# A two-layer hybrid backbone: S5 table arithmetic and its transfers put on other engines, modulation steps set after each weight chunk

## The chip, the cores and the metric

The kernel runs on one core of a Trainium2 chip. The metric is the device time of one execution in microseconds. A core has five engines that run side by side, each with a queue of its own: TensorE (PE, matmuls; PEld is its weight load), VectorE (DVE), ScalarE (ACT), GpSimd (POOL) and SyncE (SP), which here issues most transfers.

## What is computed

Two streams of 256 tokens (latents `x`, context `ctx`) of width 1024 pass through two layers. Each layer is a half-step SwiGLU feed-forward, a mixer of four branches (latent attention, Hyena convolution, S5 state space, neighbourhood attention) and a second half-step feed-forward. Every part is modulated by nine vectors that come from `c` (latents) and `c_ctx` (context):

```python
def ffn_sublayer(x, mods, base, g_pre, g_post, w_in, w_out):
    h = modulated_norm(x, g_pre, mods[base], mods[base + 1])
    return x + 0.5 * mods[base + 2] * rms_norm(swiglu(h, w_in, w_out), g_post)

mod_l = act_l @ w_mod[i] + b_mod[i]          # act_l = silu(c); 9 vectors of 1024
mod_c = act_c @ w_mod[i][:, :n_c] + b_mod[i][:n_c]   # 9 vectors in layer 0, 5 in layer 1
lam_bar = jnp.exp(lam_dt)                    # S5: powers of this make the tables
b_bar = ((lam_bar - 1.0) / lam)[..., None] * (b_re + 1j * b_im)
```

In layer 1 only the latents go through the mixer to the end, so its last four modulation vectors are needed for the latents alone.

## The kernel before

**Weight chunks.** Every weight chunk of 128 x 1024 is loaded by SP into one of four `raw` buffers and split into a high and a low part, `wh` on ScalarE (L220) and `wl` on VectorE (L221), each with three buffers. The product takes three matmuls per tile (L227 to L229). VectorE's, ScalarE's, GpSimd's and SP's instructions are put in order by a scheduler that simulates the program; only PE keeps the order of the code. `after(mark[...])` adds the rule that an instruction stands behind the marked one on its engine: `mark["wl"]` is the latest `wl`, `mark["wh"]` the latest `wh`.

**Feed-forward** (`ffn`, L533). 22 pairs of chunks, one pair a round `f`: `u[0]` and `u[1]` give the two halves, `gate` (L541 to L548) joins them on ScalarE (L543) and VectorE (L544, L545, split at L234). After each pair `step(2)` (L571) lets other work advance by two weights. The output projection calls `step(1)` after each of 16 chunks. There are four feed-forwards; three carry other work. A is layer 0's first, B layer 0's second, C layer 1's first.

**Modulation tiles** (`mod_flow`, L286). One 128 x 1024 tile of `w_mod` per step. The latents' sum is one VectorE operation (L328); the context's is a multiply on GpSimd (L332) and a sum on ScalarE (L306). In A (layer 0, vectors 2 to 8) the tiles come from SP through the same four `raw` buffers as the weights; from vector 5 on VectorE does both streams. In B and C (layer 1) they have a ring of two buffers of their own and GpSimd issues the loads (L298): vectors 0 to 4 in B, 5 to 8, latents alone, in C. In C even tiles go to VectorE, odd ones to GpSimd and ScalarE. `stepper` (L628) spreads the steps over the weights: 58 over 46 in A, 42 over 50 in B, 34 over 50 in C. In A each step also advances the Hyena filters (`hyg`, L798).

**Tables of layer 1's S5** (`s5_tables`, L1132), eight slices, 0 to 2 in B, 3 to 7 in C. `ahead` (L605) runs 4 steps a slice and 3 more over the first 15 rounds. A slice's steps:

1. On GpSimd the six small products `bb` (L1181) and the six products `wt` of 128 x 512 (L1183): the input weights.
2. On GpSimd six operations for the output vectors `vv` (L1187 to L1192); on VectorE the rotations (L1194); on ScalarE the decays (L1197). `toeplitz` of the slice before: eight small reads (L1159).
3. PE turns `wt` (L1206), ScalarE copies it to `rin`, which is stored (L1208). `keep` of the slice before (L1163).
4. PE multiplies `vv` and `bb` (L1217), which makes `strip`; `vv` is stored (L1231); the parameters of the next slice are loaded (`first`, L1146).

All transfers of this function are issued by GpSimd (`dma = G.dma_start`, L1137). Each table tile has one buffer. L205 to L210 are the six lines of the helper `cmul`, whatever engine calls it. Layer 0 makes the same tables in its own S5 part (`s5_lane`): there `wt` is made on VectorE (`prep2`) and the eight reads are issued by SP.

Of the kernel before, what the change touches and what calls it, by code (L numbers as in the profile page):

```python
# [9 lines left out]
F32 = mybir.dt.float32  # L10
# [6 lines left out]
P = 128  # L17
# [146 lines left out]
def build(tc, A):  # L164
# [20 lines left out]
    with st, tc.manual_schedule(engines={mybir.EngineType.PE}):  # L185
# [99 lines left out]
        def mod_flow(l, js, act, raw=None):  # L285

            if callable(act):
                act = act()  # L290
            tiles = [(j, k) for j in js for k in range(KT)]
            ws, back = {}, []

            def load(n):
                if n < len(tiles):
                    j, k = tiles[n]
                    ws[n] = raw() if raw else rp.tile([P, D], F32, tag="raw", name="raw")
                    (G.dma_start if raw else dma)(ws[n], A["wmod"][l, j, k])  # L298

            def finish():  # L300
                while back:
                    back.pop(0)()

            def sums(w, s, c):
                with after(mark["wh"]):
                    S.activation(w, w, AF.Copy, scale=0.5, accum_out=md[l][:, s, c : c + 1])  # L306

            def bias(j, ss):
                for s in ss:
                    m = md[l][:, s, j * KT : (j + 1) * KT]  # L310
                    V.tensor_tensor(m, m, bmt[l][:, j * KT : (j + 1) * KT], op=ALU.add)

            if raw:
                load(0)
                yield
            for n, (j, k) in enumerate(tiles):
                finish()
                load(n + 1 if raw else n)
                c = j * KT + k
                w = ws.pop(n)  # L320
                ss = [1] if l == 1 and j >= 5 else [0, 1]
                both = l == 0 and j >= JB
                fast = ss if both else [] if ss == [1] and k % 2 else [1]
                slow = [s for s in ss if s not in fast]
                for s in fast:
                    jk = sp.tile([P, D], BF16, tag="sq", name="jk", bufs=1)
                    with after(mark["wl"]):
                        V.scalar_tensor_tensor(  # L328
                            jk, w, 0.5, act[s], op0=ALU.mult, op1=ALU.mult, accum_out=md[l][:, s, c : c + 1]
                        )  # L330
                for s in slow:
                    G.tensor_tensor(w, w, act[s], op=ALU.mult)  # L332
                    back.append(lambda w=w, s=s, c=c: sums(w, s, c))
                if k == KT - 1:
                    back.append(lambda j=j, ss=ss: bias(j, ss))
                yield
            finish()

# [194 lines left out]
        def ffn(l, i, h, late, toks, nxt, gp, step, rows, fill, begun=(), xpool2=None):  # L533
# [16 lines left out]
            for f in range(NF):  # L550
                u = [new_unit(f, ab) for ab in range(2)]
                if late and f == 0:
# [11 lines left out]
                        return run  # L564

                    front([keep(u[0]), keep(u[1]), keep(u2[0])], late)
                elif late and f == 1:
                    gate(1, [pss[2], u2[1](None)])
                else:
                    gate(f, [v(None) for v in u])  # L570
                step(2)  # L571
                if f == NF - 3:
                    nxt["gr"] = rows()

# [30 lines left out]
        def ahead(stack, gp, name, slices):  # L605
# [14 lines left out]

            def go():
                f[0] += 1
                for _ in range(n * f[0] // 15 - n * (f[0] - 1) // 15):
                    next(gen, None)

            return go
# [35 lines left out]
        with ExitStack() as fs:  # L662
# [127 lines left out]
                        acts.extend(act_load())  # L790
                return acts

            st0 = stepper([(mod_flow(0, [2, 3, 4], acts0), 25), (mod_flow(0, [5, 6, 7, 8], acts0), 33)], 46, 6)

            def step0(w):
                st0(w)
                with after(mark["sp"], mark["dve"]):
                    next(hyg, None)  # L798

            late = ffn(0, 0, h, late, TALL, nxt, gp, step0, lambda: gate_rows(0, 0, 1, 0.5, [0, 1]), fill0, begun)  # L800
            h = nxt["h"]
# [2 lines left out]
        for l in range(L):  # L804
# [8 lines left out]
            with ExitStack() as fs:  # L813
# [4 lines left out]
                else:  # L818
# [6 lines left out]
                    st1 = stepper([(mod_flow(1, [0, 1, 2, 3, 4], act_load, raw1), 42)], 50, 2)  # L825
                    tg1 = ahead(fs, gp, "s5p", range(0, 3))

                    def step1(w):
# [5 lines left out]
            if not last:  # L834
                with ExitStack() as fs:
# [7 lines left out]
                    st2 = stepper([(mod_flow(1, [5, 6, 7, 8], act_load, raw2), 34)], 50, 2)  # L843
                    tg2 = ahead(fs, gp, "s5q", range(3, 8))

                    def step2(w):
# [285 lines left out]
def s5_tables(E, l, slices, tabd, sds, tp, py):  # L1132
# [10 lines left out]
    bh = lambda t, n: t.unsqueeze(2).to_broadcast([P, 4, n, 16])  # L1143
    b8 = lambda t: t.unsqueeze(3).to_broadcast([P, 4, 8, 8])
    b1 = lambda t: t.unsqueeze(2).to_broadcast([P, 4, 8, 8])
    def first(sl):  # L1146
        s5t = tp.tile([P, 4, S5_TAB], F32, tag="s5t", name="s5t")
        dma(s5t, E["s5d"][l][:, sl * 4 : sl * 4 + 4])
        prm = tp.tile([P, 5, 4, 16], F32, tag="prm", name="prm")
        dma(prm[:, 0:4], A["s5bc"][l, sl].rearrange("p a (x h) -> p a x h", h=16))  # L1150
        return s5_views(s5t), prm

    def strips(sl, strip):
# [2 lines left out]
    def toeplitz(sl):  # L1156
        tz = tp.tile([P, 4, P], F32, tag="tz", name="tz")
        for s in range(8):
            dma(tz[s * 16 : (s + 1) * 16], sds[sl][:, 0:16, (7 - s) * 16 : (7 - s) * 16 + 128].rearrange("q h d -> h q d"))  # L1159
        return tz  # L1160

    def keep(sl, tz):
# [1 line left out]

    slices = list(slices)
    s5, prm = first(slices[0])
    late = [lambda: None] * 3
    for i, sl in enumerate(slices):
        late[0]()
        rin = tp.tile([P, S5_IN], F32, tag="rin", name="rin")  # L1170
# [8 lines left out]
        h16 = lambda t: t.unsqueeze(2).to_broadcast([P, 4, 16])  # L1179
        G.tensor_scalar(prm[:, 4], prm[:, 3], -1.0, None, op0=ALU.mult)  # L1180
        cmul(G, bb[:, 0], bb[:, 1], prm[:, 0], prm[:, 1], h16(s5["kr"]), h16(s5["ki"]), tmp[:, :, 0])  # L1181
        wt = tp.tile([P, 2, 4, 8, 16], F32, tag="wt", name="wt")
        cmul(G, wt[:, 0], wt[:, 1], bk(s5["wr"], 8), bk(s5["wi"], 8), bh(bb[:, 0], 8), bh(bb[:, 1], 8), tmp[:, :, 0:8])  # L1183
        yield
        late[1]()
        vr, vi = bk(s5["vr"], 9), bk(s5["vi"], 9)
        G.tensor_tensor(vv[:, 0], vr, bh(prm[:, 2], 9), op=ALU.mult)  # L1187
        G.tensor_tensor(tmp, vi, bh(prm[:, 3], 9), op=ALU.mult)
        G.tensor_tensor(vv[:, 0], vv[:, 0], tmp, op=ALU.subtract)
        G.tensor_tensor(vv[:, 1], vr, bh(prm[:, 4], 9), op=ALU.mult)  # L1190
        G.tensor_tensor(tmp, vi, bh(prm[:, 2], 9), op=ALU.mult)
        G.tensor_tensor(vv[:, 1], vv[:, 1], tmp, op=ALU.subtract)  # L1192
        t4 = E["sp"].tile([P, 512], F32, tag="t", name="t4")[:, :256].rearrange("p (x a b) -> p x a b", a=8, b=8)
        cmul(V, rot[:, 1], rot[:, 2], b8(s5["p8r"]), b8(s5["p8i"]), b1(s5["p1r"]), b1(s5["p1i"]), t4)  # L1194
        V.tensor_scalar(rot[:, 0], rot[:, 2], -1.0, None, op0=ALU.mult)
        for d in range(2):
# [2 lines left out]
            )  # L1199
            G.memset(dec[:, d, :, :, 63 * d : 63 * d + 1], 0.0)  # L1200
        yield
        late[2]()
        for ri in range(2):
            ps = py()
            for x in range(4):
                T.transpose(ps[:, x * P : (x + 1) * P], wt[:, ri, x], ident)  # L1206
            S.activation(o["W"][:, ri], ps, AF.Copy)
        dma(tabd[0][:, sl], rin)  # L1208
        yield
        pk = py()  # L1210
        for d in range(2):
            for ri in range(2):
# [15 lines left out]
        V.scalar_tensor_tensor(  # L1228
            strip[:, 112:128], eye, d5[:, l, sl : sl + 1], strip[:, 112:128], op0=ALU.mult, op1=ALU.add
        )  # L1230
        dma(tabd[1][:, sl, :1152], vvt)  # L1231
        box = []
        late = [
            lambda sl=sl, strip=strip: strips(sl, strip),
            lambda sl=sl, box=box: box.append(toeplitz(sl)),
            lambda sl=sl, box=box: keep(sl, box[0]),
        ]
        if i + 1 < len(slices):
            s5, prm = first(slices[i + 1])
        yield  # L1240
    for f in late:
        f()
        yield

# [990 lines left out]
```

## Time and profile before

| | |
|---|---|
| median of three runs (lowest, highest) | 2654.64 us (2652.17, 2656.76) |
| the profiled execution: its time, its span | 2656.14 us, 2654.4 us |
| PE busy, matmuls | 2499.3 us (94%), 14606 |
| VectorE, ScalarE, GpSimd busy | 1719.9 (65%), 1096.1 (41%), 819.0 us (31%) |
| TensorE's granted clock, mean | 0.972 of 2.4 GHz |

Busy time is a union of an engine's instructions. "Idle before <- X" names what the wait before an instruction ended on. A busy PE is not PE at its peak, as matmuls are pipelined.

### The profile page before, as it was taken

To read this page: it belongs to the slowest core of one execution; us is meant where nothing else is said; L and a number is where in the kernel's file an instruction comes from. 1 tells how busy PE (TensorE), PEld (TensorE's weight loads), DVE (VectorE), ACT (ScalarE), POOL (GpSimd) and SP (SyncE) were. 2 spreads that over 40 slices of the span, in tenths; PEclk is the share of its full clock that TensorE was granted. 3 is DMA by queue.
4 is the path that set the end of the run, shared out by engine and by line. 5 is a ranking of instruction groups with operands and counts; after the bars stand their busy time and mean duration, and the time that the engine had idled before them with its cause. 6 is when DMAs were issued, how large, how long until landed. Compare 5 with 4: busy or idle time off the path is not lost. (4 is left out here: it accounts for less than half of the span.)

```text
span 2654.4 us, 38042 instructions
## 1 busy us (share of the span) xinstructions
PE 2499.3 (94%) x14606; PEld 2107.5 (79%) x14606; DVE 1719.9 (65%) x2544; ACT 1096.1 (41%) x1860; POOL 819.0 (31%) x844
## 2 busy tenths in 40 slices
PE   6978999999999889999899998799999999998998
PEld 3856788987788767887778887677888989997997
DVE  6788995555645898556887546564535567776564
ACT  5435323454543232444444334333324555445443
POOL 4884000100102774006975406884201011100000
PEclk8989999999999999999999999999999999999999
DMA  6345675222232233344565544655542335776564
GB/s 238 104 151 197 214 249 195 84 75 84 74 111 71 85 94 104 94 166 161 179 194 185 205 142 141 198 185 187 175 158 76 92 100 189 282 247 212 160 191 143
DMA packets 134209, 411.06 MB, mean 155 GB/s; under 512 B 27095, under 2 KB 39176, under 8 KB 131212
## 3 DMA queue, kind: packets, MB, share of 16 engines
q1 hardware_dynamic: 117388, 349.33, 40.4%
q0 software_dynamic: 16640, 59.31, 6.4%
q8 instruction: 115, 1.88, 0.3%
q14 instruction: 66, 0.54, 0.1%
HBM read 374.41 MB, written 34.16 MB: 154 GB/s over the span
## 5 line engine op out<-in xcount | busy, mean ns | idle before, releaser
L221 DVE TENSOR_TENSOR wl<-raw,wh 128x1024 fp32r<-128x1024 f32 x424 | 565.3, 1334 | 537.0 <-ACT wh L220 529.8
L220 ACT ACTIVATE wh<-raw 128x1024 fp32r<-128x1024 f32 x424 | 449.2, 1060 | 846.9 <-issue 253.8
L227 PE MATMUL pin<-hh,wh 128*128 128x512 f32 (+1 forms) x1468 | 535.9, 365 | 20.3 <-ACT wh L220 12.4
L229 PE MATMUL pin<-hh,wl 128*128 128x512 f32 (+1 forms) x1468 | 531.5, 362 | 15.4 <-DVE wl L221 15.3
L228 PE MATMUL pin<-hl,wh 128*128 128x512 f32 (+1 forms) x1468 | 531.9, 362 | 1.7 <-DVE hl L415 1.6
L246 POOL TENSOR_TENSOR r<-v,mhalf 128x1 f32<-128x1 f32 (+2 forms) x46 | 30.7, 667 | 1015.2 <-DVE v L245 916.5
L227 PEld LDWEIGHTS pin<-hh,wh 128*128 128x128 f32 x1468 | 284.9, 194 | 66.8 <-ACT wh L220 15.3
L229 PEld LDWEIGHTS pin<-hh,wl 128*128 128x128 f32 x1468 | 284.2, 194 | 60.0 <-DVE wl L221 19.1
L228 PEld LDWEIGHTS pin<-hl,wh 128*128 128x128 f32 x1468 | 284.4, 194 | 43.2 <-DVE hl L415 3.3
L1322 PE MATMUL pm<-hh,wh 128*128 128x512 f32 (+1 forms) x704 | 251.3, 357 | 0.0
L1324 PE MATMUL pm<-hh,wl 128*128 128x512 f32 (+1 forms) x704 | 245.0, 348 | 0.2 <-DVE wl L221 0.2
L1323 PE MATMUL pm<-hl,wh 128*128 128x512 f32 (+1 forms) x704 | 244.9, 348 | 0.0
L458 PE MATMUL y<-wh,gg 128*128 128x512 f32 x448 | 177.2, 396 | 0.0
L459 PE MATMUL y<-wl,gg 128*128 128x512 f32 x448 | 177.2, 396 | 0.0
L460 PE MATMUL y<-wh,gg 128*128 128x512 f32 x448 | 177.2, 396 | 0.0
L332 POOL TENSOR_TENSOR mraw<-mraw,act 128x1024 f32<-128x1024 f32 x56 | 141.2, 2522 | 57.8 <-DMA mraw<-wmod 28.2
L1322 PEld LDWEIGHTS pm<-hh,wh 128*128 128x128 f32 x704 | 134.0, 190 | 18.1 <-issue 2.5
L1324 PEld LDWEIGHTS pm<-hh,wl 128*128 128x128 f32 x704 | 133.7, 190 | 17.8 <-DVE wl L221 0.4
L1323 PEld LDWEIGHTS pm<-hl,wh 128*128 128x128 f32 x704 | 134.0, 190 | 14.9
L328 DVE SCALAR_TENSOR_TENSOR jk<-raw,act 128x1024 bf16<-128x1024 f32 x88 | 119.8, 1361 | 3.6 <-DMA raw<-wmod 2.6
L1673 POOL TENSOR_TENSOR bt<-bt,mask 128x256 f32<-128x256 f32 x32 | 25.8, 837 | 267.0 <-DMA bt<-rpb 158.9
L227 PE MATMUL pm<-hh,wh 128*128 128x256 f32 (+1 forms) x320 | 103.5, 324 | 0.0
(488 smaller groups left out, 5112.0 us busy)
## 6 DMA issues: line engine op xcount, KB each, us to landing
raw<-fin SPq DMA_DIRECT2D x176, 512.0 KB, 3.7
raw<-winf SPq DMA_DIRECT2D x122, 512.0 KB, 3.5
mraw<-wmod POOLq DMA_DIRECT2D x72, 512.0 KB, 4.8
raw<-wmod SPq DMA_DIRECT2D x64, 512.0 KB, 4.5
raw<-foa SPq DMA_DIRECT2D x64, 512.0 KB, 3.6
raw<-wbr SPq DMA_DIRECT2D x32, 512.0 KB, 3.5
raw<-fob SPq DMA_DIRECT2D x24, 512.0 KB, 4.4
s5tabd<-rin POOLq DMA_DIRECT2D x8, 1152.0 KB, 5.3
```

The costliest lines, as they stand in the source:

```text
L220: mark["wh"] = S.activation(wh, w, AF.Copy)
L221: mark["wl"] = V.tensor_tensor(wl, w, wh.bitcast(F32), op=ALU.subtract)
L227: T.matmul(out, lhsT=lh, rhs=rh, start=first and i == 0, stop=False)
L228: T.matmul(out, lhsT=lh, rhs=rl, start=False, stop=False)
L229: T.matmul(out, lhsT=ll, rhs=rh, start=False, stop=last and i == n - 1)
L332: G.tensor_tensor(w, w, act[s], op=ALU.mult)
L458: T.matmul(o, lhsT=lh, rhs=rh, start=kt == 0, stop=False)
L459: T.matmul(o, lhsT=lh, rhs=rl, start=False, stop=False)
L460: T.matmul(o, lhsT=ll, rhs=rh, start=False, stop=kt == nk - 1)
L1322: T.matmul(o, lhsT=lh, rhs=rh, start=i == 0, stop=False)
L1323: T.matmul(o, lhsT=lh, rhs=rl, start=False, stop=False)
L1324: T.matmul(o, lhsT=ll, rhs=rh, start=False, stop=i == n - 1)
```

## The change

A modulation step follows each chunk instead of each pair, at weight 1 (the skips and `ahead`'s divisor are doubled, the Hyena filters advance at every second step). In B and C the next tile's load stands behind this tile's arithmetic in the code. In layer 1's last four vectors all tiles go to VectorE. In the tables the six `wt` products go to VectorE in two steps, half of `vv` moves a step ahead, transposes and matmuls stand in one step; `first` and `toeplitz` load by SP, `rin` is stored by ScalarE's queue, `vv` is stored earlier.

```diff
@@ mod_flow
                 finish()
-                load(n + 1 if raw else n)
+                if not raw:
+                    load(n)
...
-                fast = ss if both else [] if ss == [1] and k % 2 else [1]
+                fast = ss if both else [1]
...
+                if raw:
+                    load(n + 1)
                 yield
@@ ffn
                     front([keep(u[0]), keep(u[1]), keep(u2[0])], late)
+                    step(1)
                 elif late and f == 1:
                     gate(1, [pss[2], u2[1](None)])
+                    step(1)
                 else:
-                    gate(f, [v(None) for v in u])
-                step(2)
+                    pa_ = u[0](None)
+                    step(1)
+                    gate(f, [pa_, u[1](None)])
+                step(1)
@@ ahead
-                for _ in range(n * f[0] // 15 - n * (f[0] - 1) // 15):
+                for _ in range(n * f[0] // 30 - n * (f[0] - 1) // 30):
@@ build, the skips of the three steppers
-  6, 2, 2
+  12, 4, 4 (and hyg advances at every second call of step0)
@@ s5_tables
+    scratch = lambda: E["sp"].tile([P, 512], F32, tag="t", name="t4")
+    sync = nc.sync.dma_start
     def first(sl):
...
-        dma(s5t, E["s5d"][l][:, sl * 4 : sl * 4 + 4])
+        sync(s5t, E["s5d"][l][:, sl * 4 : sl * 4 + 4])
...
-        dma(prm[:, 0:4], A["s5bc"][l, sl].rearrange("p a (x h) -> p a x h", h=16))
+        sync(prm[:, 0:4], A["s5bc"][l, sl].rearrange("p a (x h) -> p a x h", h=16))
...
-            dma(tz[s * 16 : (s + 1) * 16], sds[sl][...])
+            sync(tz[s * 16 : (s + 1) * 16], sds[sl][...])
...
-        wt = tp.tile([P, 2, 4, 8, 16], F32, tag="wt", name="wt")
-        cmul(G, wt[:, 0], wt[:, 1], ...)
-        yield
-        late[1]()
         vr, vi = bk(s5["vr"], 9), bk(s5["vi"], 9)
         (three operations for vv[:, 0], rotations, decays)
         yield
-        late[2]()
+        late[1]()
         (three operations for vv[:, 1])
+        dma(tabd[1][:, sl, :1152], vvt)
+        wt = tp.tile([P, 2, 4, 8, 16], F32, tag="wt", name="wt")
+        for part in range(2):
+            if part:
+                yield
+                late[2]()
+            tw = scratch().rearrange("p (x s h) -> p x s h", s=8, h=16)
+            with E["after"](E["mark"]["wl"]):
+                V.tensor_tensor(wt[:, part], wr, bi if part else br_, op=ALU.mult)
+                V.tensor_tensor(tw, wi, br_ if part else bi, op=ALU.mult)
+                V.tensor_tensor(wt[:, part], wt[:, part], tw, op=ALU.add if part else ALU.subtract)
+        yield
+        late[3]()
         for ri in range(2):
             (transposes of wt, copies to rin)
-        dma(tabd[0][:, sl], rin)
-        yield
+        S.dma_start(tabd[0][:, sl], rin)
         (matmuls, strip)
-        dma(tabd[1][:, sl, :1152], vvt)
```

## Rows read from the trace of the kernel before

**Rows 1.** Timeline of ScalarE, gates of A, B and C: start, us, instruction.

```profile
121.44 0.60 ACT L543 ACTIVATE t<-pin 128x512 f32<-128x512 f32 x1
...
274.03 0.58 ACT L543 ACTIVATE t<-pin 128x512 f32<-128x512 f32 x1
...
1244.13 0.58 ACT L543 ACTIVATE t<-pin 128x512 f32<-128x512 f32 x1
...
1407.87 0.58 ACT L543 ACTIVATE t<-pin 128x512 f32<-128x512 f32 x1
...
1473.28 0.58 ACT L543 ACTIVATE t<-pin 128x512 f32<-128x512 f32 x1
...
1644.00 0.58 ACT L543 ACTIVATE t<-pin 128x512 f32<-128x512 f32 x1
...
1828.59 0.58 ACT L543 ACTIVATE t<-pin 128x512 f32<-128x512 f32 x1
```

**Rows 2.** Busy time by stretch; columns PE, PEld, DVE, ACT, POOL, clock, DMA share, GB/s.

```profile
121.00:265.00 144.00, 118.81 (x469) 92.68 (x468) 120.40 (x147) 62.83 (x94) 99.99 (x76) 0.91 0.50 167
1244.00:1408.00 164.00, 152.01 (x742) 123.99 (x741) 132.55 (x137) 69.72 (x113) 130.06 (x123) 0.96 0.59 195
1644.00:1829.00 185.00, 160.32 (x820) 129.69 (x819) 105.44 (x125) 59.54 (x98) 143.26 (x177) 0.93 0.58 189
```

**Rows 3.** Waits of PE, first 1205 to 1400, then 1600 to 1870: us, times, longest.

```profile
PE pn L1217 <- POOL vvt L1192: 7.9, 2, 6.5
...
PE pn L1206 <- POOL wt L210: 4.1, 2, 3.8
...
PE pn L1206 <- POOL wt L210: 14.0, 3, 6.5
PE pn L1217 <- POOL vvt L1189: 8.4, 1, 8.4
```

**Rows 4.** Waits of SP's queue, 120 to 265.

```profile
SPq L176 <- ACT raw L306: 63.8, 12, 13.4
```

**Rows 5.** Lines of GpSimd by form, 1195 to 1930: busy us, mean ns, idle before.

```profile
L332 POOL TENSOR_TENSOR mraw<-mraw,act 128x1024 f32<-128x1024 f32 x56 | 141.2, 2522 | 57.8 <-DMA mraw<-wmod 28.2 <-DVE jk L328 21.5 <-DMA act<-actd 3.5
L298 POOL DMA_DIRECT2D mraw<-wmod x72 | 41.1, 571 | 125.4 <-ACT mraw L306 107.2 <-DVE jk L328 6.8 <-DMA mraw<-wmod 4.8
L1159 POOL DMA_DIRECT2D tz<-s5sd x64 | 32.7, 519 | 2.8 <-DMA s5sd<-strip 2.6
L210 POOL TENSOR_TENSOR wt<-wt,tmp 128x512 f32<-128x512 f32 x8 | 12.5, 1567 | 0.3
...
L205 POOL TENSOR_TENSOR wt<-s5t,bb 128x512 f32<-128x512 f32 x8 | 10.0, 1252 | 0.0
```

**Rows 6.** Lines of VectorE by form, layer 0's own S5, 860 to 1060.

```profile
L208 DVE TENSOR_TENSOR wt<-s5t,bb 128x512 f32<-128x512 f32 x8 | 10.5, 1318 | 0.0
...
L210 DVE TENSOR_TENSOR wt<-wt,t 128x512 f32<-128x512 f32 x8 | 5.4, 680 | 0.0
```

**Rows 7.** Timeline of VectorE in B: start, us, instruction, idle before.

```profile
1243.22 1.22 DVE L221 TENSOR_TENSOR wl<-raw,wh 128x1024 fp32r<-128x1024 f32 x1 [1.23 <-ACT wh L220]
...
1267.09 4.42 DVE L221 TENSOR_TENSOR wl<-raw,wh 128x1024 fp32r<-128x1024 f32 x1 [0.74 <-ACT wh L220]
```

**Rows 8.** Timeline of GpSimd in B.

```profile
1213.32 1.16 POOL L1187 TENSOR_TENSOR vvt<-s5t,prm 128x576 f32<-128x576 f32 x1
...
1216.68 1.24 POOL L205 TENSOR_TENSOR wt<-s5t,bb 128x512 f32<-128x512 f32 x1
...
1266.74 2.40 POOL L332 TENSOR_TENSOR mraw<-mraw,act 128x1024 f32<-128x1024 f32 x1
```

**Rows 9.** The ring's tile in B, 1206 to 1600: ns min/median/max, first and last start.

```profile
L328 DVE SCALAR_TENSOR_TENSOR jk<-mraw,act x40: 1207/1218/2194, 1235.1 to 1508.2; 128x1024 bf16<-128x1024 f32 x40
...
DMA to landing us min/median/max: 3.7/4.7/6.5
```

**Rows 10.** The Toeplitz tile in layer 0, 860 to 1060, its reads by SP.

```profile
L176 SPq DMA_DIRECT2D tz<-sd x64: 303/424/1672, 895.3 to 1043.7; - x64
```

More of the change, by code (lines that the diff above doesn't have):

```diff
@@ L791, in acts0 @@
                 return acts
-            st0 = stepper([(mod_flow(0, [2, 3, 4], acts0), 25), (mod_flow(0, [5, 6, 7, 8], acts0), 33)], 46, 6)
+            st0 = stepper([(mod_flow(0, [2, 3, 4], acts0), 25), (mod_flow(0, [5, 6, 7, 8], acts0), 33)], 46, 12)
+            half = [0]
             def step0(w):
                 st0(w)
-                with after(mark["sp"], mark["dve"]):
-                    next(hyg, None)
+                half[0] += 1
+                if half[0] % 2 == 0:
+                    with after(mark["sp"], mark["dve"]):
+                        next(hyg, None)
             late = ffn(0, 0, h, late, TALL, nxt, gp, step0, lambda: gate_rows(0, 0, 1, 0.5, [0, 1]), fill0, begun)
@@ L824, in build @@
                     x1, raw1 = mod_ring(fs, "mrB")
-                    st1 = stepper([(mod_flow(1, [0, 1, 2, 3, 4], act_load, raw1), 42)], 50, 2)
+                    st1 = stepper([(mod_flow(1, [0, 1, 2, 3, 4], act_load, raw1), 42)], 50, 4)
                     tg1 = ahead(fs, gp, "s5p", range(0, 3))
@@ L842, in build @@
                     x2, raw2 = mod_ring(fs, "mrC")
-                    st2 = stepper([(mod_flow(1, [5, 6, 7, 8], act_load, raw2), 34)], 50, 2)
+                    st2 = stepper([(mod_flow(1, [5, 6, 7, 8], act_load, raw2), 34)], 50, 4)
                     tg2 = ahead(fs, gp, "s5q", range(3, 8))
@@ L1158, in toeplitz @@
         for s in range(8):
-            dma(tz[s * 16 : (s + 1) * 16], sds[sl][:, 0:16, (7 - s) * 16 : (7 - s) * 16 + 128].rearrange("q h d -> h q d"))
+            sync(tz[s * 16 : (s + 1) * 16], sds[sl][:, 0:16, (7 - s) * 16 : (7 - s) * 16 + 128].rearrange("q h d -> h q d"))
         return tz
@@ L1166, in s5_tables @@
     s5, prm = first(slices[0])
-    late = [lambda: None] * 3
+    late = [lambda: None] * 4
     for i, sl in enumerate(slices):
@@ L1181, in s5_tables @@
         cmul(G, bb[:, 0], bb[:, 1], prm[:, 0], prm[:, 1], h16(s5["kr"]), h16(s5["ki"]), tmp[:, :, 0])
-        wt = tp.tile([P, 2, 4, 8, 16], F32, tag="wt", name="wt")
-        cmul(G, wt[:, 0], wt[:, 1], bk(s5["wr"], 8), bk(s5["wi"], 8), bh(bb[:, 0], 8), bh(bb[:, 1], 8), tmp[:, :, 0:8])
-        yield
-        late[1]()
         vr, vi = bk(s5["vr"], 9), bk(s5["vi"], 9)
@@ L1189, in s5_tables @@
         G.tensor_tensor(vv[:, 0], vv[:, 0], tmp, op=ALU.subtract)
[L1190 to L1193, printed above, removed]
+        t4 = scratch()[:, :256].rearrange("p (x a b) -> p x a b", a=8, b=8)
         cmul(V, rot[:, 1], rot[:, 2], b8(s5["p8r"]), b8(s5["p8i"]), b1(s5["p1r"]), b1(s5["p1i"]), t4)
@@ L1201, in s5_tables @@
         yield
-        late[2]()
+        late[1]()
+        G.tensor_tensor(vv[:, 1], vr, bh(prm[:, 4], 9), op=ALU.mult)
+        G.tensor_tensor(tmp, vi, bh(prm[:, 2], 9), op=ALU.mult)
+        G.tensor_tensor(vv[:, 1], vv[:, 1], tmp, op=ALU.subtract)
+        dma(tabd[1][:, sl, :1152], vvt)
+        wt = tp.tile([P, 2, 4, 8, 16], F32, tag="wt", name="wt")
+        wr, wi, br_, bi = bk(s5["wr"], 8), bk(s5["wi"], 8), bh(bb[:, 0], 8), bh(bb[:, 1], 8)
+        for part in range(2):
[9 more added lines that the diff above has]
+        late[3]()
         for ri in range(2):
@@ L1235, in s5_tables @@
             lambda sl=sl, box=box: box.append(toeplitz(sl)),
+            lambda: None,
             lambda sl=sl, box=box: keep(sl, box[0]),
@@ L1240, in s5_tables @@
         yield
-    for f in late:
+    for f in (late[0], late[1], late[3]):
         f()
```

## The prediction, made before the changed kernel ran

> **What bounds the kernel now.** I read the busy time by stretches first, then PE's waits, then the lines of the engine that those name, and last the queues that the change touches. Three stages matter, each a feed-forward of 22 pairs of weight chunks: A (layer 0, first), B (layer 0, second) and C (layer 1, first). In A modulation tiles run beside the pairs, in B and C modulation tiles and the tables of layer 1's S5.
>
> TensorE sets the pace where nothing holds it: the last six pairs of B take from 1407.87 to 1473.28, that is 10.90 us a pair [rows 1]. The first thirteen pairs after B's start take 163.74 us, C's 184.59, against 13 x 10.90 = 141.7. The stretches say why [rows 2]: PE is busy 152.0 of 164 us in B and 160.3 of 185 in C, so it is idle 12.0 and 24.7. Its granted clock falls to 0.96 and 0.93 of 2.4 GHz, so some matmuls run at 1.2 GHz behind each pause; if all of that came back it would be 0.04 x 152 = 6.1 us and 0.07 x 160 = 11.2. The idle part has a name [rows 3]: in B 7.9 + 4.1 = 12.0 us are waits of the tables' matmuls and transposes for GpSimd (`vvt`, `wt`), which is all of it; in C the two longest such rows give 22.4 of 24.7. So at most 12.0 + 6.1 = 18.1 us can come out of B and 24.7 + 11.2 = 35.9 out of C. What stands between these and the gate rows (22.0 and 42.9 above the pace) is PE's own work on the tables, which stays.
>
> GpSimd is late because it has too much to do: 130.1 of 164 us in B and 143.3 of 185 in C [rows 2], the rest of the time standing before a load or a multiply whose partner isn't ready.
>
> A loses time in another way. From pair 5 to pair 14 it takes 152.6 us where nine pairs need 98.1 [rows 1], part of that for the Hyena filters' matmuls. SP, which issues the weights' loads, stands 63.8 us for ScalarE's sums to free a modulation tile [rows 4]: tiles and weight chunks share four buffers, and two or three tiles stand in a row between two pairs. VectorE is busy 120.4 of 144 us there [rows 2], so no more than 23.6 us can come back, whatever order is chosen.
>
> **The change, part by part.** *Input weights to VectorE.* Six multiply-adds per slice leave GpSimd; the six groups run from 10.0 to 12.5 us for 8 slices, 67.3 in all, 8.4 a slice [rows 5]. *Transfers.* Eight Toeplitz reads go to SP, 32.7 / 8 = 4.1 us a slice; two parameter loads go to SP and the `rin` store to ScalarE's queue, three issues at some 0.57 [rows 5], 1.7. Together 14.2 us a slice leave GpSimd: 43 us of 130 in B (3 slices), 71 of 143 in C (5). GpSimd would be busy about 87 of 154 us in B and 72 of 158 in C. *Tables' order.* The first output vector is now made in the step of the inputs, the second in the next, and the weights in two halves; transposes and the matmuls for `strip` both stand in the fourth step. In C two steps used to fall on one pair in half of the pairs, so that transposes stood right behind the multiply; now one half-pair at least lies between any two. Both waits of [rows 3] lose their cause twice, by less work and by distance.
>
> VectorE pays. The trace of before shows the same six multiplies on VectorE in layer 0's own S5: groups from 5.4 to 10.5 us for 8 slices [rows 6], 46.8 in all, 5.85 a slice. That is the value I take, since GpSimd worked beside it there too; undisturbed it would be 6 x 0.68 = 4.1 (the smallest group). In B 3 x 5.85 = 17.6 us come on top of 132.6, so 150 of the 154 us that I leave; in C 29.3 on 105.4.
>
> The other end of the price is a block. An undisturbed `wl` takes 1.22 us, and 4.42 when it starts at 1267.09 [rows 7] beside a GpSimd multiply that starts at 1266.74 and takes 2.40 [rows 8]. If each of the six stood out a multiply of 2.52 us [rows 5], a slice would cost 6 x (0.68 + 2.52) = 19.2 us. I stay with 5.85, because layer 0's row is the same operation in the same form; the block is the far end, and it decides rival 1. The Trainium skill, "SBUF — State Buffer", section "SBUF: two separate sides", says that a VectorE operation with two SBUF inputs and a GpSimd operation that reads SBUF exclude each other for the whole instruction. The `wl` row agrees; taken at its worst, that rule speaks against this part of the change, for the sum by it would be 19.2 us a slice and no gain.
>
> *Latents' vectors.* In C every second tile of the last four vectors went by GpSimd (2.52 us) and ScalarE; 16 more now go to VectorE at 1.22 [rows 5, 9], 19.5 us in all. C has 1.36 tiles a pair (34 steps over 50 weights, two weights a pair), so 18 fall into the 13 pairs and about 9 of them are new: 10.8 us. VectorE in C: 105.4 + 29.3 + 10.8 = 145.5 of 158 us. Both stages fit, C with more room, and less GpSimd work shortens VectorE's blocks.
>
> *SP.* A slice brings ten issues. The eight Toeplitz reads take 0.42 us each on SP in layer 0, 1.67 at worst [rows 10]: 3.4 to 13.4 us a slice. They cost nothing while weights are loaded ahead: three pairs of split buffers and four raw ones stand before PE, some two chunks of 5.45 us. Should SP stand for the strip's landing beyond that, PE waits (rival 2). *ScalarE's queue* gets eight stores. No row shows an issue there; between nothing (the engine is idle for more than half of each stretch [rows 2]) and GpSimd's 0.57 it is 4.6 us in all, with ScalarE's own copies as the only thing queued behind. I take nothing.
>
> *The ring's load behind the multiply.* Tiles of B and C have two buffers. The load of the next tile now comes behind this tile's multiply in the code. GpSimd's queue isn't in the code's order: at 1213.32 it runs a `vvt` multiply that the code has behind the `wt` multiply of 1216.68 [rows 8]. So the swap changes a precedence, not a chain; I take nothing, and rival 3 prices the chain.
>
> *Steps after each chunk.* The same tiles over the same weights, one or two at a time where two or three stood together. This is what can help A, and nothing in the rows says by how much: above is VectorE's idle 23.6 us, below a loss of the same kind if a weight chunk falls behind a tile twice as often, which I bound at 10. I take 8, a third of the upper end, as VectorE is the nearer limit.
>
> **Sum.** The profiled execution took 2656.1 us. B: 10 of 18.1, since VectorE would be full. C: 27 of 35.9, three quarters. A: 8. Together 45, so 2611; the median of the three runs is 1.5 us below that execution, so **2610 us**.
>
> **Rivals.** 1. *VectorE becomes the bound*, 0.16. In B nothing is gained when a slice costs (164 - 132.6) / 3 = 10.5 us, between 5.85 and 19.2. C at that price needs 105.4 + 52.5 + 10.8 = 169 us and gains 16; A half of its 8. That is 2656 - 20 = 2636. For it: B's 150 of 154. Against: GpSimd's share falls by a third to a half.
>
> 2. *Weights wait behind the tables' reads on SP*, 0.08. Eight slices at 3.4 us uncovered give back 27 of the 45: 2638. Against: in A SP stands 63.8 us for a buffer [rows 4], so its queue has room to issue in.
>
> 3. *Slower: the ring paces VectorE*, 0.10. If GpSimd keeps the code's order, a tile of B is a chain: multiply 2.4, landing 4.7, vector 1.2 [rows 5, 9], 8.3 us. B has 42 steps over 50 weights, 1.68 tiles a pair, so 13.9 us a pair instead of 10.90, with `wl` queued behind each late vector. Twenty pairs lose 3.0 each, 60 us, where B now loses 18: 42 worse. With C's 27 and A's 8 gained it is 7 worse, 2663, median 2662. It decides once the chain is longer than 10.90 / 1.68 = 6.5 us. For it: tiles follow each other at 273 / 39 = 7.0 us now [rows 9], already over that. Against: the order of [rows 8].
>
> 4. *The order in the code reaches no queue* (A gains nothing, the loads as before): 2618, within the forecast's range.
>
> **Numbers.** Forecast with rival 4: 0.62. Rivals 1 and 2: 0.24. Rival 3: 0.10. The remaining 0.04 is a gain eaten by small new stalls. A measurement here tells about 0.2%, 5 us. Faster by more: 0.62 + 0.24 less a little, 0.85; same 0.05; slower 0.10. The range runs from nearly all bounds met (18 + 36 + 22 = 76, 2580) to a little short of no change, 2650; it leaves out rival 3.
>
> **What would show it.** Right: no wait of the tables' matmuls and transposes for GpSimd in B and C, thirteen pairs at about 154 and 158 us, clock near 1.00, `wt` on VectorE at 4 to 6 us a slice. B unchanged with PE waiting for `wl` means rival 1; ScalarE waiting for weights to land behind SP, rival 2; VectorE standing for the ring's loads, rival 3. The forecast is wrong if PE's waits in B and C stay above 20 us together, or if A loses over 10 us.

## The result and the profile after

The changed kernel takes **2599.45 us** (median of 4 runs, 2597.24 to 2601.43) against 2655.13 for the kernel before, run beside it: a ratio of 0.9785, 95% interval 0.9773 to 0.9798 (the two medians divide to 0.9790, inside it). The forecast was 2610, with 2580 to 2650 as its range. The profiled execution took 2597.24 us, its span is 2595.4 and its granted clock 0.982. GpSimd is busy 671.6 us where it was 819.0, VectorE 1750.1 where it was 1719.9, and PE has the same 14606 matmuls.

The gates of the three stages on ScalarE's timeline (start, us, instruction), answering to [rows 1]: pairs 5 and 14 of A, pairs 2, 15 and 21 of B, pairs 2, 15 and 21 of C.

```profile
121.39 0.60 ACT L546 ACTIVATE t<-pin 128x512 f32<-128x512 f32 x1
...
266.03 0.58 ACT L546 ACTIVATE t<-pin 128x512 f32<-128x512 f32 x1
...
1232.20 0.58 ACT L546 ACTIVATE t<-pin 128x512 f32<-128x512 f32 x1
...
1390.43 0.57 ACT L546 ACTIVATE t<-pin 128x512 f32<-128x512 f32 x1
...
1453.06 0.58 ACT L546 ACTIVATE t<-pin 128x512 f32<-128x512 f32 x1
...
1617.54 0.58 ACT L546 ACTIVATE t<-pin 128x512 f32<-128x512 f32 x1
...
1769.44 0.58 ACT L546 ACTIVATE t<-pin 128x512 f32<-128x512 f32 x1
...
1834.80 0.58 ACT L546 ACTIVATE t<-pin 128x512 f32<-128x512 f32 x1
```

A's nine pairs took 152.6 us and now take 144.6, B's thirteen 163.7 and now 158.2, C's thirteen 184.6 and now 151.9. From one gate to another, the whole gain of 59.0 us of span comes apart as follows. The last column has the same differences read on TensorE itself, as explained below the table.

| stretch | before | after | difference | on TensorE |
|---|---|---|---|---|
| A, pairs 0 to 21 | 282.5 | 276.8 | -5.7 | -7.4 |
| A's end to B's first gate | 872.2 | 867.1 | -5.1 | -3.4 |
| B, pairs 0 to 21 | 246.8 | 237.5 | -9.3 | -9.3 |
| B's end to C's first gate | 153.2 | 147.9 | -5.3 | -6.1 |
| C, pairs 0 to 21 | 267.5 | 233.9 | -33.6 | -32.8 |

What lies ahead of A and behind C is the same in sum. Of the five rows, the second and the fourth stand in no term of the prediction.

A gate is ScalarE's instruction and can stand behind other work of ScalarE's queue, so it is not always a mark of TensorE's pace. TensorE's own mark is a pair's first matmul: a pair has 48 matmuls of L227 to L229, counted back from the last one ahead of the output projection. The last column runs from the first matmul of pair 2 to the last of pair 21. Pairs 2 and 15 of B begin, before the change and then after it:

```profile
1236.66 0.39 PE L227 MATMUL pin<-hh,wh 128*128 128x512 f32 x1
...
1401.49 0.39 PE L227 MATMUL pin<-hh,wh 128*128 128x512 f32 x1
...
1225.78 0.39 PE L227 MATMUL pin<-hh,wh 128*128 128x512 f32 x1
...
1381.28 0.39 PE L227 MATMUL pin<-hh,wh 128*128 128x512 f32 x1
```

On TensorE B's thirteen pairs took 164.8 us and now take 155.5, which is 9.3 less where the gates show 5.5. The gate of pair 15 now comes 9.15 us after that pair's first matmul (before: 6.38), as ScalarE's queue first serves a sum that stood for GpSimd's multiply:

```profile
1387.90 1.06 ACT L306 ACTIVATE mraw<-mraw 128x1024 f32<-128x1024 f32 x1 [2.61 <-POOL mraw L333]
```

In C both readings agree (184.7 and 151.9 us on TensorE). Where they differ by more than 1 us below, both are given.

Busy time by stretch, columns as in [rows 2] (PE, PEld, DVE, ACT, POOL, clock, DMA share, GB/s):

```profile
121.00:266.00 145.00, 123.14 (x486) 95.54 (x485) 122.92 (x152) 66.41 (x100) 105.73 (x79) 0.92 0.49 170
1232.00:1391.00 159.00, 154.35 (x761) 125.81 (x760) 143.12 (x153) 70.36 (x114) 101.48 (x84) 0.99 0.61 201
1617.00:1770.00 153.00, 153.00 (x830) 126.39 (x829) 119.12 (x165) 51.92 (x82) 65.53 (x94) 1.00 0.71 233
```

C's stretch has no idle time of PE at all, at a clock of 1.00: the pairs and the tables' own matmuls fill it. In B PE is idle 4.7 us, and the view of PE's waits from 1232 to 1391 holds one row. From 1617 to 1770 it is empty. Nothing of [rows 3] is left.

```profile
PE pin L229 <- DVE wl L221: 4.7, 5, 2.1
```

VectorE's lines for the weights (the products `wt` of the tables), first in B (1214 to 1400, three slices), then in C (1600 to 1870, five): busy us, mean ns, idle before.

```profile
L1224 DVE TENSOR_TENSOR wt<-wt,t 128x512 f32<-128x512 f32 x6 | 9.6, 1593 | 0.2
L1223 DVE TENSOR_TENSOR t<-s5t,bb 128x512 f32<-128x512 f32 x6 | 6.1, 1021 | 0.2
L1222 DVE TENSOR_TENSOR wt<-s5t,bb 128x512 f32<-128x512 f32 x6 | 4.3, 718 | 0.0
...
L1222 DVE TENSOR_TENSOR wt<-s5t,bb 128x512 f32<-128x512 f32 x10 | 9.0, 906 | 5.7 <-POOL bb L207 5.7
L1223 DVE TENSOR_TENSOR t<-s5t,bb 128x512 f32<-128x512 f32 x10 | 6.9, 687 | 0.1
...
L1224 DVE TENSOR_TENSOR wt<-wt,t 128x512 f32<-128x512 f32 x10 | 6.8, 683 | 0.1
```

A slice costs VectorE 20.0 / 3 = 6.67 us in B and 22.7 / 5 = 4.54 in C.

SP's waits, in A (120 to 265) and in C (1617 to 1770). The first answers to [rows 4]; the second says that SP does stand for the strip's landing, up to 9.6 us at a time, while PE waits for nothing.

```profile
SPq L176 <- ACT raw L306: 57.8, 14, 7.3
...
SPq L1173 <- DMA s5sd<-strip: 37.7, 5, 9.6
```

### The profile page after: what moved, and what is told of

It reads as the page before. It is cut to its first block, busy times and chain, and to the rows that moved or that the text cites. A ratio compares the mean times of both kernels' runs of the same rounds, so it can differ in the third digit from the quotient of the medians.

```text
span 2595.4 us, 38077 instructions
## 1 busy us (share of the span) xinstructions
PE 2482.5 (96%) x14606; PEld 2096.0 (81%) x14606; DVE 1750.1 (67%) x2624; ACT 1079.3 (42%) x1828; POOL 671.6 (26%) x692
## 5 line engine op out<-in xcount | busy, mean ns | idle before, releaser
L221 DVE TENSOR_TENSOR wl<-raw,wh 128x1024 fp32r<-128x1024 f32 x424 | 557.1, 1314 | 468.2 <-ACT wh L220 461.4
L229 PE MATMUL pin<-hh,wl 128*128 128x512 f32 (+1 forms) x1468 | 529.9, 361 | 18.7 <-DVE wl L221 18.6
L227 PE MATMUL pin<-hh,wh 128*128 128x512 f32 (+1 forms) x1468 | 531.6, 362 | 11.8 <-DVE hh L415 7.8
L229 PEld LDWEIGHTS pin<-hh,wl 128*128 128x128 f32 x1468 | 282.5, 192 | 64.7 <-DVE wl L221 24.9
L227 PEld LDWEIGHTS pin<-hh,wh 128*128 128x128 f32 x1468 | 282.8, 193 | 56.9 <-DVE hh L415 9.4
L333 POOL TENSOR_TENSOR mraw<-mraw,act 128x1024 f32<-128x1024 f32 x40 | 102.6, 2565 | 49.6 <-DVE jk L329 48.3
L227 PE MATMUL pm<-hh,wh 128*128 128x256 f32 (+1 forms) x320 | 103.5, 324 | 0.0
L228 PE MATMUL pm<-hl,wh 128*128 128x256 f32 (+1 forms) x320 | 102.7, 321 | 0.1
```

Of the source, the lines that this page charges most:

```text
L221: mark["wl"] = V.tensor_tensor(wl, w, wh.bitcast(F32), op=ALU.subtract)
L227: T.matmul(out, lhsT=lh, rhs=rh, start=first and i == 0, stop=False)
L228: T.matmul(out, lhsT=lh, rhs=rl, start=False, stop=False)
L229: T.matmul(out, lhsT=ll, rhs=rh, start=False, stop=last and i == n - 1)
```

## The experiments

The numbers of each are compared by ratio to the kernel before, which ran beside it; times of pairs are read from the trace of one execution of each kernel, from the gates or on TensorE, as above.

### Which part brought it

**Steps alone**: the kernel before, with nothing but the steps after each chunk (and the skips, the divisor and the Hyena filters' every second step that go with them).

```
                 else:
-                    gate(f, [v(None) for v in u])
-                step(2)
+                    pa_ = u[0](None)
+                    step(1)
+                    gate(f, [pa_, u[1](None)])
+                step(1)
```

> The kernel before with nothing but the steps after each chunk. If GpSimd's load is what held B and C (my theory), the steps alone are worth what stage A gained, 8 to 11 us of 2655, so 2644 to 2647, and the waits of the tables' matmuls and transposes for GpSimd in B and C stay above 25 us together. If it is the distance between the tables' steps (rival), the waits in C fall under 10 us and the time to some 2625.

Measured: 2657.29 us, ratio 0.9997 (0.9988 to 1.0007): no change, where 2644 to 2647 was expected. A's nine pairs take 144.3, so the 8 us of A are there, and B begins 7.6 earlier. But B's pairs 2 to 15 take 168.7 (before 163.7; on TensorE 169.0 and 164.8) and C's 189.9 (before 184.6). The waits of [rows 3] stay, with 15.0 us in B and 27.9 in C; C's longest, from 1640 to 1831:

```profile
PE pn L1214 <- POOL wt L210: 13.2, 3, 6.1
PE pn L1225 <- POOL vvt L1197: 9.7, 1, 9.7
```

With the tables late as they were, the steps in smaller portions cost 4.2 us in B and 5.3 in C on TensorE, and what A gains is given back.

**Everything but the steps**: the changed kernel, steps after each pair.

```
-                    pa_ = u[0](None)
-                    step(1)
-                    gate(f, [pa_, u[1](None)])
-                step(1)
+                    gate(f, [v(None) for v in u])
+                step(2)
```

> The changed kernel with the steps after each pair again. By load: only A's gain goes, 8 to 11 us, so 2608 to 2611, C's thirteen pairs stay near 152 us. By distance: C's waits for GpSimd or VectorE come back with over 10 us as two table steps share a pair, 2620 or more.

Measured: 2614.28 us, ratio 0.9835 (0.9821 to 0.985), some 3 us above the range that was expected by load. A's pairs are back at 152.6 and B begins 9.2 later than in the changed kernel. C takes 154.3, 2.4 more than with the steps. B's gates show 155.8, 2.4 *less*, but that is the late gate of pair 15: on TensorE B takes 156.9, 1.4 more. So the steps are worth about 0.5% in the changed kernel, most of it in A, and nothing in the kernel before.

**Order and steps, no work moved**: the changed kernel with weights, transfers, latents and the ring's load where they were. Its core (the weights' products go back to GpSimd as in the square below):

```
-    sync = nc.sync.dma_start
+    sync = G.dma_start
...
-        S.dma_start(tabd[0][:, sl], rin)
+        dma(tabd[0][:, sl], rin)
...
-                if not raw:
-                    load(n)
+                load(n + 1 if raw else n)
...
-                fast = ss if both else [1]
+                fast = ss if both else [] if ss == [1] and k % 2 else [1]
...
-                if raw:
-                    load(n + 1)
```

> The kernel before with the steps after each chunk and the tables' new order (first vector, second vector, weights in two halves, transposes in the fourth step), but weights on GpSimd, transfers on GpSimd, latents and the ring's load as before. It stands between the run with the steps alone (2657.3, ratio 0.9997) and the changed kernel. My theory (two causes: GpSimd's amount of work, and the distance between a table's arithmetic and PE's use of it): the order alone gives less than half of B and C, since 130 and 143 us of GpSimd work stay: B 160 to 167, C 175 to 188, in all 2632 to 2652. Rival (distance alone did it): waits of the tables' matmuls below 6 us in both stages, B below 160 and C below 162, in all 2605 to 2620.

Measured: 2652.77 us, ratio 0.9985 (0.9975 to 0.9994). B takes 168.6, as with the steps alone (168.7; on TensorE 169.0 in both), C 182.7 (189.9). PE's waits, first B from 1235 to 1404, then C from 1640 to 1823:

```profile
PE pn L1225 <- POOL wt L1219: 17.4, 3, 7.2
...
PE pn L1225 <- POOL wt L1219: 22.8, 6, 8.0
```

The weights now stand half a pair or more ahead of the transposes in the code, and GpSimd is still 7 to 8 us late with them. Distance in the code is no distance in time on a queue that is behind. The rival, that distance alone did it, falls; my own figures were still too hopeful, 160 to 167 for B where order alone gives nothing, and 2652 at most. In C the order is worth 7 us beside the steps (190.0 against 182.7 on TensorE), even with GpSimd late.

**Weights alone**: the kernel before with the six multiply-adds on VectorE, in the old place.

```
-        cmul(G, wt[:, 0], wt[:, 1], bk(s5["wr"], 8), bk(s5["wi"], 8), bh(bb[:, 0], 8), bh(bb[:, 1], 8), tmp[:, :, 0:8])
+        tw = E["sp"].tile([P, 512], F32, tag="t", name="t4").rearrange("p (x s h) -> p x s h", s=8, h=16)
+        cmul(V, wt[:, 0], wt[:, 1], bk(s5["wr"], 8), bk(s5["wi"], 8), bh(bb[:, 0], 8), bh(bb[:, 1], 8), tw)
```

> The kernel before with the weights' six multiply-adds on VectorE and nothing else: order of the tables, transfers, latents, ring and steps as before. If taking 8.4 us a slice off GpSimd is what counts: C at 154 to 165 against 184.6, B at 156 to 162 against 163.7, A unchanged at 152.6, in all 2615 to 2630. If the distance between arithmetic and transposes is needed as well: waits of the transposes for wt remain, now for VectorE, above 8 us in C, and C stays above 168, in all 2632 to 2650.

Measured: 2625.33 us, ratio 0.9872 (0.9857 to 0.9887). This one edit gives 1.28 of the 2.15%. B's thirteen pairs take 153.1, less than in the changed kernel; C's 163.1, which is 21.5 of the 32.7 us gained there. PE's waits in B (1244 to 1398) and C (1632 to 1796):

```profile
PE pin L229 <- DVE wl L221: 3.2, 2, 2.4
...
PE pn L1207 <- DVE wt L207: 5.3, 1, 5.3
PE pn L1207 <- DVE wt L210: 4.0, 1, 4.0
```

In C the transposes still wait 9.3 us for `wt`, now from VectorE, and the clock there is 0.97. Both waits fall in one slice (transposes at 1723.84 and 1728.94). VectorE and then GpSimd ahead of them:

```profile
1720.29 0.69 DVE L206 TENSOR_TENSOR t<-s5t,bb 128x512 f32<-128x512 f32 x1 [3.37 <-POOL bb L210]
...
1715.77 4.14 POOL L1159 DMA_DIRECT2D tz<-s5sd  x8
1719.92 0.33 POOL L210 TENSOR_TENSOR bb<-bb,tmp 128x64 f32<-128x64 f32 x1
```

VectorE stood 3.37 us for `bb`, which GpSimd made behind eight Toeplitz issues of 4.14 us. So GpSimd is still late in C, busy 111 of 163 us. All but the steps together took C to 154.3, 8.8 us less. What did that is not separated: in the old order the transfers on GpSimd stand in this wait, while in the new order the same transfers on GpSimd cost C's pairs 0.1 us (152.0, below). Either the new order or moving the transfers may be enough; no run moved the transfers in the old order. B needed neither: on TensorE it takes 151.9 us here, less than in the changed kernel.

### Weights and transfers, a square

Three kernels put back on GpSimd the weights, the tables' transfers, and both; with the changed kernel they make a square.

```
-            tw = scratch().rearrange("p (x s h) -> p x s h", s=8, h=16)
-            with E["after"](E["mark"]["wl"]):
-                V.tensor_tensor(wt[:, part], wr, bi if part else br_, op=ALU.mult)
-                V.tensor_tensor(tw, wi, br_ if part else bi, op=ALU.mult)
-                V.tensor_tensor(wt[:, part], wt[:, part], tw, op=ALU.add if part else ALU.subtract)
+            G.tensor_tensor(wt[:, part], wr, bi if part else br_, op=ALU.mult)
+            G.tensor_tensor(tmp[:, :, 0:8], wi, br_ if part else bi, op=ALU.mult)
+            G.tensor_tensor(wt[:, part], wt[:, part], tmp[:, :, 0:8], op=ALU.add if part else ALU.subtract)
```

> The changed kernel with the six input-weight products of a slice on GpSimd, in the same two steps. GpSimd gets 8.4 us a slice back: B 101 + 25 = 126 of 159 us, about the share it had before, C 66 + 42 = 108 of 153. My theory: B's waits for GpSimd return with 5 to 12 us, C's with less than 8, so 2605 to 2615. Rival (VectorE is the bound in B): PE's 4.7 us of waits for wl in B go and nothing takes their place, 2592 to 2598.

```
-    sync = nc.sync.dma_start
+    sync = G.dma_start
...
-        S.dma_start(tabd[0][:, sl], rin)
+        dma(tabd[0][:, sl], rin)
```

> The changed kernel with all of the tables' transfers issued by GpSimd again. Ten issues on SP and one on ScalarE go back, 5.8 us a slice: B 101 + 17 = 118 us, C 66 + 29 = 95. My theory: room is left, 0 to 6 us slower, 2599 to 2606. Rival (weights wait behind the tables' reads on SP): faster by some us, and ScalarE's waits for weights get shorter.

Both edits at once:

> The changed kernel with the weights on GpSimd and all of the tables' transfers on GpSimd's queue, so that only the tables' order, the steps after each chunk, the latents' vectors and the ring's load are new. It is the fourth corner of a square with the changed kernel (B 158.2, C 151.9), weights back alone (161.9, 160.9) and transfers back alone (158.4, 152.0). My theory (GpSimd's amount of work decides, and either part takes it below the point where it is late): the corner loses far more than the two parts added, B 165 to 169 and C 170 to 183, 2630 to 2650. Rival (the parts add up): B 162 and C 161, some 2615 to 2622.

| on GpSimd | us, ratio (interval) | B, 13 pairs (on TensorE) | C, 13 pairs |
|---|---|---|---|
| neither (the change) | 2599.45, 0.9785 (0.9773 to 0.9798) | 158.2 (155.5) | 151.9 |
| transfers | 2605.89, 0.9813 (0.9797 to 0.9829) | 158.4 (157.4) | 152.0 |
| weights | 2612.57, 0.9830 (0.9816 to 0.9845) | 161.9 (158.4) | 160.9 |
| both | 2638.81, 0.9923 (0.9907 to 0.9940) | 169.3 (169.6) | 177.0 |

Seen from the last row, moving the transfers saves 11.2 us in B (on TensorE) and 16.1 in C, moving the weights 12.2 and 25.0, moving both 14.1 and 25.1. The two don't add up: once the weights are gone, the transfers are worth 1.9 and 0.1 us in the pairs. So GpSimd's amount of work decides, up to the point where it is in time; what is taken off beyond that point buys little or nothing there.

With the weights alone back on GpSimd, PE's waits in B (1232 to 1391) are these:

```profile
PE pin L229 <- DVE wl L221: 4.9, 3, 3.5
PE pn L1228 <- POOL wt L1222: 2.0, 1, 2.0
```

The wait for GpSimd is 2.0 us, where 5 to 12 was expected. PE's wait for `wl` is as long as in the changed kernel (4.7), though VectorE has six products a slice less: so these waits are not the price of the products alone.

The transfers are still worth 6 us in the whole, and the place is mainly the front of B and of C, where the rows are normalised ahead of the first gate: on TensorE the stretch ahead of B is 3.7 us longer than in the changed kernel, the one ahead of C 3.8. Two views of the run with the transfers on GpSimd, VectorE and GpSimd before B's first pair (start, us, instruction):

```profile
1207.82 0.66 DVE L245 SCALAR_TENSOR_TENSOR v<-ss 128x1 f32<-128x1 f32 x1 [0.90 <-ACT sq L380]
...
1210.46 0.52 DVE L386 TENSOR_SCALAR xn<-xr,r 128x512 f32<-128x512 f32 x1 [1.99 <-POOL r L246]
```

```profile
1207.30 1.16 POOL L1197 TENSOR_TENSOR vvt<-s5t,prm 128x576 f32<-128x576 f32 x1
1208.40 0.10 POOL L1207 MEMSET rin<- 128x4 f32 x1
1208.47 1.16 POOL L1210 TENSOR_TENSOR vvt<-s5t,prm 128x576 f32<-128x576 f32 x1
1209.59 0.31 POOL L207 TENSOR_TENSOR bb<-bb,tmp 128x64 f32<-128x64 f32 x1
1209.87 0.56 POOL L246 TENSOR_TENSOR r<-v,mhalf 128x1 f32<-128x1 f32 x1
```

`r` is the power -1/2 of one number a row, 0.56 us on GpSimd, and the whole front waits for it. `v` is there at 1208.48; `r` begins at 1209.87, behind the first slice's vectors. In the changed kernel's GpSimd the same two multiplies are done by 1202.14, and `r` finds its queue empty:

```profile
1200.97 1.17 POOL L1210 TENSOR_TENSOR vvt<-s5t,prm 128x576 f32<-128x576 f32 x1
1202.11 0.81 POOL L207 TENSOR_TENSOR bb<-bb,tmp 128x64 f32<-128x64 f32 x1
1205.16 0.57 POOL L246 TENSOR_TENSOR r<-v,mhalf 128x1 f32<-128x1 f32 x1 [2.24 <-DVE v L245]
```

PE's wait for `xn` in B's front is 6.2 or 6.3 us in the six kernels with these transfers on GpSimd's queue (before, steps alone, weights alone, order and steps, both back, and this one), and 3.9 to 4.3 in the eight that have them on SP. That the transfers decide is shown by these runs; that it works through the queue position of `r` is read from the rows, as no run moved `r` itself.

### The small parts

**Latents' vectors** back on GpSimd and ScalarE for every second of the last four tiles.

```
-                fast = ss if both else [1]
+                fast = ss if both else [] if ss == [1] and k % 2 else [1]
```

> The changed kernel with one thing back: the odd one of the last four vectors' tiles is multiplied on GpSimd and summed on ScalarE again. Only stage C holds such tiles. My theory (GpSimd's overload is gone, so C has room on both engines): C's pairs 0 to 21 take 217 to 222 us against 217.3 of the changed kernel, no wait of the tables' matmuls for GpSimd above 3 us, in all 2599 to 2605. Rival (GpSimd has no room for these 2.5 us multiplies beside the tables): waits for vvt or for the tiles come back and C loses 8 us or more, 2607 to 2620.

Measured: 2602.47 us, ratio 0.9798 (0.978 to 0.9815), C's pairs unchanged at 151.9 (2 to 15) and 217.3 (2 to 21, which the expectation calls 0 to 21). The 3 us more lie between B and C (151.2 against 147.9), and there again `r` stands in a queue, in C's front on GpSimd of this run:

```profile
1589.53 2.85 POOL L333 TENSOR_TENSOR mraw<-mraw,act 128x1024 f32<-128x1024 f32 x1
1592.35 0.76 POOL L207 TENSOR_TENSOR bb<-bb,tmp 128x64 f32<-128x64 f32 x1
1593.07 0.56 POOL L246 TENSOR_TENSOR r<-v,mhalf 128x1 f32<-128x1 f32 x1
```

PE waits 5.3 us for `xn` there, 2.9 in the changed kernel. The two intervals overlap, so the size of this part in the whole is not settled.

**The ring's load** ahead of the arithmetic again.

```
-                if not raw:
-                    load(n)
+                load(n + 1 if raw else n)
...
-                if raw:
-                    load(n + 1)
```

> The changed kernel with one thing back: the load of the ring's next tile stands ahead of this tile's arithmetic. My theory (the swap changes a precedence, not a chain): 2597 to 2602, pairs of B and C within 2 us of 158.2 and 151.9. The rival of the prediction in which the ring paces VectorE: with the load first the chain of a tile is shorter, B gains 4 us or more, 2590 to 2596.

Measured: 2600.78 us, ratio 0.9787 (0.9771 to 0.9802), B 156.2 (on TensorE 153.8), C 152.0: the same within the interval, as the prediction's zero for it had it.

### VectorE's room

**The products made twice** on VectorE, nothing else changed.

```
                 V.tensor_tensor(wt[:, part], wt[:, part], tw, op=ALU.add if part else ALU.subtract)
+            with E["after"](E["mark"]["wl"]):
+                V.tensor_tensor(wt[:, part], wr, bi if part else br_, op=ALU.mult)
+                V.tensor_tensor(tw, wi, br_ if part else bi, op=ALU.mult)
+                V.tensor_tensor(wt[:, part], wt[:, part], tw, op=ALU.add if part else ALU.subtract)
```

> The changed kernel, with the six products of a slice's input weights made twice on VectorE, one after the other, so that a slice costs VectorE 13.3 us in B and 9.1 in C (twice 6.67 and 4.54). The prediction's bound for VectorE in B was 10.5 us a slice: B had 158.2 us with 143 of 159 us busy, so 20 more go over the span. If VectorE is the bound in B: pairs 2 to 15 at 166 to 175 us, waits of PE for wl above 10 us, C nearly unchanged (119 of 153 busy, so 152 to 156), in all 2609 to 2622. If VectorE's busy time still has cover in B: pairs within 3 us, 2598 to 2603.

Measured: 2620.52 us, ratio 0.986 (0.9843 to 0.9878). B takes 166.7 us (on TensorE 163.3), about as much as before the change, with PE waiting 10.8 us for `wl`; C takes 165.8, where 152 to 156 was expected. PE's waits, B from 1233 to 1401, then C from 1626 to 1793:

```profile
PE pin L229 <- DVE wl L221: 10.8, 5, 3.2
...
PE pn L1234 <- DVE wt L1228: 8.9, 4, 3.5
```

In B VectorE sets what is lost, as expected, at some 11 us a slice (33.7 / 3, the sum of the six lines of these products from 1214 to 1400): 13.7 us more of its work cost about 8 us. In C it isn't full (136.8 of 167 us from 1626 to 1793): there PE waits for `wt`, which the second round makes later, and the clock falls to 0.97.

**Two slices in B and six in C**, and then one and seven, instead of three and five.

```
-                    tg1 = ahead(fs, gp, "s5p", range(0, 3))
+                    tg1 = ahead(fs, gp, "s5p", range(0, 2))
...
-                    tg2 = ahead(fs, gp, "s5q", range(3, 8))
+                    tg2 = ahead(fs, gp, "s5q", range(2, 8))
```

> The changed kernel with two slices' tables in B and six in C, where three and five stood. B's VectorE was busy 143 of 159 us and PE still waited 4.7 us for wl, C's 119 of 153 with no wait of PE at all. If VectorE's slices are what is left in B: wl waits below 2 us there, B's pairs 2 to 15 at 152 to 156, C's at 151 to 155 (TensorE's own work for one more slice), in all 2594 to 2599. Rival (the work only moves, since TensorE must do it in either stage): 2598 to 2602, same.

> As the run with two and six slices, with one in B and seven in C. If C's cover holds: one more slice's gain in B of 1 to 4 us and none lost in C, 2592 to 2599. If C has no room for seven (tables that took to 1770 of 1835 us with five slices would take to 1826 by 28 us a slice, at its very end): PE waits for the last tables behind C, 2600 to 2615.

Measured: 2598.2 us, ratio 0.9774 (0.9758 to 0.979), and 2611.7, ratio 0.9822 (0.9807 to 0.9837). With two and six B falls to 145.3 and C rises to 164.2. On TensorE B goes from 155.5 to 145.6: the waits of 4.7 us are gone, the clock is 1.00 where it was 0.99, and 40 of the tables' 120 matmuls in these pairs moved with the slice. Six slices are 27 steps over 30 half-pairs where five were 23; the steps follow each other more closely, and in C (1610 to 1775) transposes wait for VectorE:

```profile
PE pn L1230 <- DVE wt L1224: 6.3, 3, 3.3
```

With one and seven (31 steps) these waits are 11.9 us and the time rises. Two and six is a draw with the change, not a version shown to be better.

## Why the prediction was right, and where not

**The sum.** The forecast was 45 us off the profiled execution, 59 came. By the gates the terms held 48.6 of them: A 5.7 (forecast 8), B 9.3 (10), C 33.6 (27); on TensorE 49.5: 7.4, 9.3 and 32.8. The other 10 us lie between the stages, which the prediction costed at nothing. Of these the waits for `xn` explain 2.0 (6.2 to 4.2) ahead of B and 5.2 (8.1 to 2.9) ahead of C. On TensorE 1.4 is left ahead of B and 0.9 ahead of C; the first is less than the 2.7 us by which five kernels with nearly the same code there differ (875.8 to 878.5 us).

**A: 8.** The nine pairs gave 8.0. The whole stage gave 5.7 by the gates, as pairs 14 to 21 take 2.2 us more there, and 7.4 on TensorE. The bound came from a row, the third of it that was taken from none, so that the size came out is luck; that the steps do it is shown by the run with the steps alone. SP's wait for ScalarE's sums fell from 63.8 to 57.8 and its longest from 13.4 to 7.3 [rows 4]: it comes in smaller portions, and most of it is still there. What the prediction did not see is that the same edit works in B and C too: while the tables were late it cost 4.2 and 5.3 us on TensorE, and in the changed kernel it gains 1.4 and 2.4.

**B: 10.** Right in sum. The mechanism too: weights alone remove the waits for GpSimd. But "two ways at once, less work and distance" was wrong for B: distance alone gave nothing there. And the thirteen pairs took 158.2 by the gates and 155.5 on TensorE where 154 stood: of rival 1 its sign came in part. VectorE is busy 143 of 159 us, PE waits 4.7 us for `wl`, and the doubled products show that little room is left. A slice's price was 6.67 us where 5.85 was taken, well short of rival 1's 10.5. With the weights alone B took 151.9 on TensorE, 3.6 less than with the whole change. The steps don't explain that (without them it is 156.9); whether the new order or what came with it does stays open.

**C: 27.** The mis-sized term. Three quarters of the bound was a guess at what would be left, and nothing was: 32.7 of 35.9 us came out of thirteen pairs, with no wait of PE and a clock of 1.00. VectorE's sum was too high, 145.5 forecast against 119.1 measured: the weights cost 4.54 a slice, not 5.85, and only four of the five slices' products fall into these pairs (18.7 us where the sum had 29.3). The work that VectorE had before got shorter too: a `wl` took 1346 ns in the mean of these thirteen pairs, where it had taken 1608, and the 13 splits of L234 took 9.1 us instead of 15.6. GpSimd was busy 65.5 us beside it, where 72 was forecast and 143 had been.

**The price of `wt`.** Nearest row, 5.85; measured 6.67 and 4.54; far end by a block at every product, 19.2. In C the products run at 683 to 906 ns, and in B one line has a mean of 1593. Single blocks of the kind that [rows 7] shows do occur, but few: six of the 48 products took more than 1 us, 1.66 to 2.77. One of them, beside GpSimd's multiply, in B of the changed kernel:

```profile
1285.31 2.84 POOL L333 TENSOR_TENSOR mraw<-mraw,act 128x1024 f32<-128x1024 f32 x1 [0.84 <-DVE md L311]
...
1285.93 2.77 DVE L1224 TENSOR_TENSOR wt<-wt,t 128x512 f32<-128x512 f32 x1
```

The product ends 0.55 us after the multiply. The rule of the Trainium skill, "SBUF — State Buffer", section "SBUF: two separate sides", agrees with such single rows; the sum at its worst, every product standing out a GpSimd multiply, is not what these traces show.

**Rival 2** is visible and harmless: SP stands 37.7 us for strips in C, and PE waits for nothing. ScalarE's queue cost nothing that shows. **Rival 3** did not come: VectorE waits 9.9 us in B for the ring's loads, but it waited 10.6 before the change, and the load's place makes no difference that can be measured. **Rival 4**, that the order in the code reaches no queue, is wrong for A, whose gain goes with the steps alone.

## What to carry to other kernels

When an engine is late with a product, take work off it before you change the order: new order and steps without it gave 0.15%, the weights alone 1.28%. What else had to change for C's last 9 us was not separated. Before you read a small difference from a mark on one engine, look at the engine whose time counts: the gates on ScalarE showed 2.4 us against the steps in B where TensorE had 1.4 us for them. Moves that relieve the same engine don't add up; measure the corner with both undone before you credit either. A term for "what comes back" should include the stretches between the stages, where a small operation on the relieved engine may stand on the path.

## What was not expected

- A 0.56 us operation on 128 numbers on GpSimd stands on the path to the start of B and of C: where it queues behind a 1.16 us product PE waits 6.2 us for `xn`, otherwise 4.2; behind a 2.85 us multiply 5.3 instead of 2.9.
- Smaller portions of side work are no gain in themselves: the same edit took 8.0 us from A's nine pairs and added 4.2 and 5.3 (on TensorE) to B's and C's thirteen, as long as GpSimd was late.
- In C, doubling 4.5 us of VectorE work a slice (22.7 us over the stage) cost 13.9 us in thirteen pairs though VectorE was busy only 82% of them: its products came late to one consumer, and TensorE's granted clock went from 1.00 to 0.97.
